# Attention of a decoder trunk: ScalarE takes all its parts of a projection's bank and of a turned bank first, then VectorE its own

## The chip, the cores and the metric

One core of a Trainium2 chip runs the whole kernel. The metric is the device time of one execution in microseconds, lower is better. A core has five engines with queues of their own that run in order: TensorE (PE), VectorE (DVE), ScalarE (ACT), GpSimd (POOL) and SyncE (SP, which here issues DMAs). They wait for each other by semaphores.

## The reference

One layer of a hybrid decoder trunk: 1024 tokens, model width 1024, float32. A normed input is projected for three groups of heads (a short convolution, attention of 8 heads of 64, a spatial gating MLP); their outputs go through `w_out`, then come a feed-forward MLP with squared ReLU (4096 wide) and a gated per-layer input. The part that matters here is the attention, which has no softmax:

```
q, k: RMSNorm per head of the projected columns; v as projected
z = einsum('bqhd,bkhd->bhqk', q, k) * scale          # scale = 64 ** -0.5
log_beta = log_sigmoid(z)
log_rem  = where(causal, log_sigmoid(-z), 0)         # strictly causal
suffix   = cumsum(log_rem, reverse=True) - log_rem
weights  = where(causal, exp(log_beta + suffix), 0)
o = einsum('bhqk,bkhd->bqhd', weights, v)
```

## The kernel before

Every float32 operand of a large product is split into a high part (rounded by ScalarE) and a low part (source minus high, by VectorE): `split`, L135 to L143. A product is three matmuls, high by high, high by low and low by high (L165 to L167).

**Order.** The program is written as generators that are woven together: attention of one pair of heads with the projection of the next, in the ratio of their matmuls (`weave`); a short piece can be queued to come some units of work later (`later`). On top of that a scheduler built into the framework simulates the program and sets the order of each engine's queue from it. So moving a line can move what stands around it on every engine.

**Stages** (us of the profiled execution): input, gating and its weights up to about 76; the projection of the first head pair to about 117; attention woven with the projections of pairs 1 to 3 up to about 330; attention of the last pair woven with the convolution to about 420; out-projection to about 505; then the feed-forward MLP and the gate to the end.

**`project(pr)`**, L343 to L391. For each of the 8 tiles of 128 tokens, 24 matmuls write q, k and v of two heads into one PSUM bank, `qkv_ps` (128x384). These banks come from `ps_mm`, which has two, so the matmuls of a tile wait until the tile two before it has been read out. The readers are, in the order of the lines: ScalarE squares q and k (L374, tile `qk_sq`, or `sq`), VectorE sums the squares (`ss`, L377), GpSimd raises them to the power -1/2 (`rs`, L174 in a helper), VectorE scales q and k (`qk`, L382), then ScalarE takes v's high part (`V`, L141 in `split`) and VectorE its low part (L142). The last one frees the bank. Where engines read one bank after another, semaphores between them keep that order.

**`turn_qk`**, L393 to L417, queued after every second tile: transposes of `qk` into a bank of `ps_tr` (`qk_tr`; three banks, shared with the transposed weights `w_tr`), which is read out as q's high part (`QS`, ScalarE), q's low part (`q_lo`, VectorE), k's high part (`KH`, ScalarE, L405) and k's low parts of the two heads (`KL`, VectorE, L407, twice).

**`attend(pr)`**, L421 to L523. `stick`: for each block of 128 queries, z by three kinds of matmul (L447 with KH, L449 with KL, L453 for the mask) into banks of `ps_z` (two), two sigmoids on ScalarE (`rem` L454, `wt` L455), a running product on VectorE (a scan of up to 1024 elements, L459), and weights `wt` times `rem` (L462; on VectorE for the blocks 3, 5 and 7, on GpSimd for the rest). `gather`: the weights are transposed (`w_tr`, L484), split (`wT_hi` on ScalarE, `wT_lo` on VectorE, L138 and L139) and multiplied with V (`av`, L502). Each head has four groups `g` of two blocks; the two heads of a pair run them upwards, then downwards, so that the largest groups of the two heads meet.

Of the kernel before, what the change touches and what calls it, by code (L numbers as in the profile page):

```python
# [8 lines left out]
F32R = mybir.dt.float32r  # L9
AF = mybir.ActivationFunctionType  # L10
ALU = mybir.AluOpType
AX = mybir.AxisListType

P = 128
# [4 lines left out]
HD = 64  # L19
# [13 lines left out]
def hybrid_block(ctx: ExitStack, tc: tile.TileContext, a: dict):  # L33
# [5 lines left out]
    nc = tc.nc  # L39
# [17 lines left out]
    def name(s):  # L57
        n_of[0] += 1
        return f"{s}_{n_of[0]}"

    def slot(s, dt=F32, shape=(P, HT)):
        return sp.tile(list(shape), dt, tag="slot", name=name(s))
# [16 lines left out]
    def half_tmp(s, shape=(P, 256)):  # L79
        return tp.tile(list(shape), F32, tag="half", name=name(s), bufs=3)  # L80

    def bank(pool, s):
        return pool.tile([P, HT], F32, tag=pool.name, name=name(s))
# [4 lines left out]
    def wide_bank(s):  # L88

        turn_of[0] ^= 1  # L90
        return bank((ps_mm, ps_z)[turn_of[0]], s)
# [3 lines left out]
    def block(t):  # L95

        return t // 4, slice(t % 4 * P, (t % 4 + 1) * P)
# [21 lines left out]
    def load_const(key, shape):  # L119
        t = const.tile(list(shape), F32, name=f"c_{key}")  # L120
        nc.gpsimd.dma_start(t, a[key])
        return t
# [6 lines left out]
    gq = load_const("gq", [P, 1])  # L129
# [5 lines left out]
    def split(src, hi, lo, scale=None, low=nc.vector):  # L135

        if scale is None:
            last_hi[0] = nc.scalar.copy(hi, src)  # L138
            low.tensor_tensor(out=lo, in0=src, in1=hi, op=ALU.subtract)  # L139
        else:  # L140
            nc.scalar.activation(hi, src, AF.Copy, scale=scale)  # L141
            nc.vector.scalar_tensor_tensor(out=lo, in0=src, scalar=scale, in1=hi,  # L142
                                           op0=ALU.mult, op1=ALU.subtract)  # L143

    def load_w(src, cols, low=nc.vector):

        st = stage(src, cols)
        hi = wp.tile([P, 384], F32R, tag="w", name=name("whi"))
        lo = wp.tile([P, 384], F32R, tag="w", name=name("wlo"))
        split(st, hi[:, :cols], lo[:, :cols], low=low)  # L150
        return hi, lo
# [9 lines left out]
    def product(ps, terms, first=True, last=True):  # L161


        for i, ((lh, ll), (rh, rl)) in enumerate(terms):
            nc.tensor.matmul(ps, lh, rh, start=first and i == 0, stop=False)  # L165
            nc.tensor.matmul(ps, lh, rl, start=False, stop=False)  # L166
            done = nc.tensor.matmul(ps, ll, rh, start=False, stop=last and i == len(terms) - 1)  # L167
        return done

    def cols(parts, sl):  # L170
        return parts[0][:, sl], parts[1][:, sl]

    def power_mhalf(out, in_, n):
        last_power[0] = nc.gpsimd.tensor_tensor(out=out, in0=in_, in1=mhalf[:, :n], op=ALU.pow)  # L174
# [40 lines left out]
    ms1e, r1, r1h = [], [], []  # L215
# [27 lines left out]
    def later(units, piece):  # L243

        waiting.append((emitted[0] + units, piece))
# [97 lines left out]
    def project(pr):  # L343

        wk = [load_w(a["w_qkv"][pr, k], 384, nc.gpsimd if pr and k % 2 == 0 else nc.vector)
              for k in range(KT)]

        QS = [[None, None], [None, None]]

        KH = [[None, None], [None, None]]  # L350
        KL = [[None, None], [None, None]]
        V = [None] * 4
        low_q = [None, None]
        heads[pr] = QS, KH, KL, V, low_q
        for t in range(KT):
            th, ts = block(t)
            if t % 4 == 0:
                for hh, other in enumerate((hi_p, lo_p)):
                    KL[hh][th] = slot("KL", F32R)
                    nc.gpsimd.memset(KL[hh][th][other].bitcast(F32), 0.0)  # L360
                KH[0][th] = slot("KH", F32R)
                QS[0][th] = slot("QS", F32R)
                low_q[th] = slot("q_lo", F32R)
                QS[1][th] = slot("QS", F32R)
                KH[1][th] = slot("KH", F32R)
            ps = bank(ps_mm, "qkv_ps")[:, :384]
            for k0 in range(0, KT, 2):
                product(ps, [(cols(xn[k][th], ts), wk[k]) for k in (k0, k0 + 1)],
                        k0 == 0, k0 == KT - 2)
                yield 18  # L370

            sq = half_tmp("qk_sq", (P, 4, HD + 1))
            nc.scalar.copy(sq[:, :, HD], ms1e[t].broadcast_to([P, 4]))
            nc.scalar.activation(sq[:, :, :HD], ps[:, :256].rearrange("p (h d) -> p h d", d=HD),  # L374
                                 AF.Square, scale=HD ** -0.5)
            ss = small.tile([P, 4], F32, tag="ss", name=name("ss"))
            nc.vector.tensor_reduce(out=ss, in_=sq, axis=AX.X, op=ALU.add)  # L377
            rs = small.tile([P, 4], F32, tag="rs", name=name("rs"))
            power_mhalf(rs, ss, 4)
            if t % 2 == 0:  # L380
                qk = tp.tile([P, 2, 256], F32, tag="qk", name=name("qk"), bufs=2)
            nc.vector.tensor_tensor(  # L382
                out=qk[:, t % 2].rearrange("p (h d) -> p h d", d=HD),
                in0=ps[:, :256].rearrange("p (h d) -> p h d", d=HD),
                in1=rs.unsqueeze(2).broadcast_to([P, 4, HD]), op=ALU.mult)
            if t % 2 == 0:
                V[t // 2] = slot("V", F32R, (P, 2, 2, 2, HD))
            v = V[t // 2][:, t % 2]
            split(ps[:, 256:].rearrange("p (h d) -> p h d", d=HD), v[:, :, 0], v[:, :, 1], scale=r1[t])
            if t % 2 == 1:  # L390
                later(72, lambda t=t, qk=qk: turn_qk(heads[pr], t, qk))  # L391

    def turn_qk(head, t, qk):  # L393

        QS, KH, KL, _, low_q = head
        th = t // 4
        tr = bank(ps_tr, "qk_tr")
        for i in range(2):
            for j in range(2):
                o = j * 256 + i * P  # L400
                nc.tensor.transpose(tr[:, o:o + P], qk[:, i, j * P:(j + 1) * P], ident)
        ws = slice((t % 4 - 1) * P, (t % 4 + 1) * P)

        split(tr[:, :256], QS[0][th][:, ws], low_q[th][:, ws], scale=gq)
        nc.scalar.activation(KH[0][th][:, ws], tr[:, 256:], AF.Copy, scale=gk)  # L405
        for hh, own in enumerate((lo_p, hi_p)):
            nc.vector.scalar_tensor_tensor(out=KL[hh][th][own, ws], in0=tr[own, 256:],  # L407
                                           scalar=gk[own], in1=KH[0][th][own, ws],
                                           op0=ALU.mult, op1=ALU.subtract)
        if t % 4 == 3:  # L410
            nc.scalar.copy(KH[1][th][hi_p], KH[0][th][hi_p])
            nc.scalar.copy(KH[1][th][lo_p], KH[0][th][hi_p])
            nc.scalar.copy(KH[0][th][hi_p], KH[0][th][lo_p])
            nc.vector.tensor_copy(QS[1][th][hi_p], QS[0][th][hi_p])
            nc.vector.tensor_copy(QS[1][th][lo_p], low_q[th][hi_p])
            nc.vector.tensor_copy(QS[0][th][hi_p], low_q[th][lo_p])
        return 8  # L417
# [263 lines left out]
    for n in range(KT):  # L681
# [5 lines left out]
        for h in range(2):  # L687
            ps = wide_bank("pp_ps")
# [4 lines left out]
    for _ in normalize(1):  # L693
        pass
    alone = stream(gating(), project(0))
    fill = stream(project(1), project(2), project(3), convolve())
    for _ in alone:
        pass
# [48 lines left out]
    ps = ctx.enter_context(tc.tile_pool(name="ps", bufs=8, space=PSUM, reuse_waits="tile"))  # L747

    def late_slot(tag, s, dt=F32):
        return late.tile([P, HT], dt, tag=tag, name=name(s), bufs=LATE[tag])  # L750
# [172 lines left out]
    for h in range(2):  # L923
        for n in (0, 4, 1, 5, 2, 6, 3, 7):
# [28 lines left out]
            t = hg[n][h] = late_slot("tmp", "hg")  # L953
# [29 lines left out]
    for i in range(FT):  # L983
# [16 lines left out]
        v = late_slot("tmp", "v")  # L1000
# [104 lines left out]
    def residual(n, h):  # L1105
        if h_res[n][h] is None:
            h_res[n][h] = slot("h")
            nc.sync.dma_start(h_res[n][h], h_dram[n, h])
        return h_res[n][h]
# [28 lines left out]
    for s, (c, p, j) in enumerate(steps):  # L1138
# [13 lines left out]
        elif p == 6:  # L1152
            subtract(nc.vector, u_sum[j], u_sum[j], bank)
            if last:
                add(nc.vector, h_res[j][1], h_res[j][1], u_sum[j])
                for h in range(2):
                    t = residual(j + 4, h)
                    subtract(nc.vector, t, t, u_sum[j])
        elif p in (2, 3):
            t = residual(j, p - 2)  # L1160
# [3 lines left out]
        else:  # L1164
            h = 0 if p == 4 else 1
            t = residual(j + 4, h)
# [55 lines left out]
    for p in GATE:  # L1222
        for j in range(4):
# [14 lines left out]
            for bank, c in zip(banks, cs):  # L1238
# [8 lines left out]
                elif p == 5:  # L1247
                    e_of[j] = late_slot("tmp", "e")
                    add(nc.vector, e_of[j], bank, v_of[j])
                    t = late_slot("tmp", "gt")  # L1250
                    add(nc.vector, t, d_bank.pop((3, j))[0], e_of[j])
                    gated(j, 1, t, t, c, by_dma=True)
                elif p == 7:
                    t = e_of[j][:, c]
                    add(nc.vector, t, bank, t)
                    gated(j + 4, 1, t, t, c, -1.0, True)
                elif p == 4:
                    t = v_of[j][:, c]
# [84 lines left out]
```

## Time and profile before

| | before |
|---|---|
| time, median of 3 runs (range) | 1217.78 us (1216.59 to 1219.84) |
| the profiled execution: time, span | 1216.81 us, 1214.9 us |
| mean granted TensorE clock | 0.993 |
| DMA moved, mean rate | 254.04 MB, 209 GB/s |

The span runs from the first to the last instruction. The rows of the profile name an instruction by its engine, line, operation and tiles (output, then inputs); a row of the timeline gives start, duration and, in brackets, the idle time ahead of it with the instruction that ended it. L numbers are lines of the kernel before; in the kernel after, lines from 394 to 404 are 4 higher and later ones 6 higher.

### The profile page before, as it was taken

What the parts mean: (1) busy time and instruction counts of PE and PEld (TensorE: products, weight loads), DVE (VectorE), ACT (ScalarE), POOL (GpSimd) and SP (SyncE); (2) the same over time, 40 slices, a digit from 0 to 9 for tenths busy, and PEclk for the clock granted to TensorE, in tenths of its full rate; (3) what the DMA queues carried; (4) which work ended last, traced back from release to release, by engine and by line L of the source; (5) the groups of instructions that cost most, each with busy time, mean ns of one, the idle gap of its engine ahead of it and who ended that gap; (6) DMA issues with size and microseconds to landing.
All of it is one profiled execution on the core that took longest, in us unless ns stands there. A gap on an engine that the chain in (4) does not pass through costs nothing.

```text
span 1214.9 us, 17743 instructions
## 1 busy us (share of the span) xinstructions
PE 1191.8 (98%) x5852; PEld 1018.2 (84%) x5852; DVE 886.8 (73%) x1310; ACT 629.1 (52%) x1244; POOL 400.9 (33%) x408
## 2 busy tenths in 40 slices
PE   9999899999999999999999999999999999999997
PEld 7899899898988888888888888888888888888886
DVE  7846888988887657877878768787665556753597
ACT  7736767667764355744333333356443444546542
POOL 3324345365343312124453544421023301013412
PEclk9999999999999999999999999999999999999998
DMA  9602359999554786779999899778889985654857
GB/s 318 222 18 94 124 166 267 247 184 171 132 116 101 164 287 207 198 194 269 251 256 251 231 261 258 217 249 277 321 248 313 279 264 171 217 163 112 179 160 208
DMA packets 127964, 254.04 MB, mean 209 GB/s; under 512 B 14496, under 2 KB 22432, under 8 KB 127168
## 3 DMA queue, kind: packets, MB, share of 16 engines
q1 hardware_dynamic: 94992, 168.08, 41.8%
q0 software_dynamic: 27664, 57.05, 25.0%
q10 hardware_dynamic: 5216, 27.79, 6.4%
q8 instruction: 46, 0.75, 0.2%
q14 instruction: 46, 0.38, 0.1%
HBM read 192.30 MB, written 92.80 MB: 235 GB/s over the span
## 4 chain that ended last, share of the span: by engine, by line
PE 86%; DVE 5%; DMA 4%; POOL 1%; issue 1%; ACT 1%; SPq 0%; ACTq 0%; DVEq 0%; POOLq 0%
PE f_ps L812 25%; PE d_ps L812 25%; PE g_ps L812 6%; PE qkv_ps L165 3%; PE qkv_ps L166 3%; PE qkv_ps L167 3%; PE av L502 2%; PE w_tr L484 2%; DVE rem L459 1%; PE vu_ps L167 1%; PE vu_ps L166 1%; PE vu_ps L165 1%; PE o_ps L167 1%; PE o_ps L165 1%; PE o_ps L166 1%
## 5 line engine op out<-in xcount | busy, mean ns | idle before, releaser
L139 DVE TENSOR_TENSOR w_lo<-raw,w_hi 128x512 fp32r<-128x512 f32 x280 | 245.1, 879 | 88.1 <-ACT w_hi L138 86.4
L138 ACT CAST w_hi<-raw 128x512 fp32r<-128x512 f32 x280 | 171.9, 619 | 232.6 <-PE d_ps L812 112.6
L812 PE MATMUL f_ps<-hn_hi,w_hi 128*128 128x512 f32 x448 | 175.1, 392 | 0.0
L812 PE MATMUL d_ps<-f_hi,w_hi 128*128 128x512 f32 x448 | 174.8, 390 | 0.0
L812 PE MATMUL f_ps<-hn_lo,w_hi 128*128 128x512 f32 x448 | 174.7, 390 | 0.0
L812 PE MATMUL f_ps<-hn_hi,w_lo 128*128 128x512 f32 x448 | 174.5, 390 | 0.0
L812 PE MATMUL d_ps<-f_hi,w_lo 128*128 128x512 f32 x448 | 174.3, 389 | 0.0
L812 PE MATMUL d_ps<-f_lo,w_hi 128*128 128x512 f32 x448 | 174.3, 389 | 0.0
L459 DVE TENSOR_TENSOR_SCAN rem<-rem 128x128 f32<-128x128 f32 (+3 forms) x64 | 90.2, 1420 | 23.0 <-ACT rem L454 22.9
L812 PEld LDWEIGHTS f_ps<-hn_lo,w_hi 128*128 128x128 f32 x448 | 84.4, 188 | 17.9 <-issue 0.2
L812 PEld LDWEIGHTS f_ps<-hn_hi,w_hi 128*128 128x128 f32 x448 | 84.5, 189 | 17.6 <-issue 0.2
L812 PEld LDWEIGHTS f_ps<-hn_hi,w_lo 128*128 128x128 f32 x448 | 84.4, 188 | 17.7
L812 PEld LDWEIGHTS d_ps<-f_hi,w_hi 128*128 128x128 f32 x448 | 84.1, 188 | 17.7 <-issue 0.2
L812 PEld LDWEIGHTS d_ps<-f_lo,w_hi 128*128 128x128 f32 x448 | 84.1, 188 | 17.6 <-issue 0.2
L812 PEld LDWEIGHTS d_ps<-f_hi,w_lo 128*128 128x128 f32 x448 | 84.1, 188 | 17.5
L165 PE MATMUL qkv_ps<-whi,xn_hi 128*128 128x384 f32 x256 | 90.4, 353 | 0.1
L167 PE MATMUL qkv_ps<-whi,xn_lo 128*128 128x384 f32 x256 | 87.8, 343 | 0.0
L166 PE MATMUL qkv_ps<-wlo,xn_hi 128*128 128x384 f32 x256 | 87.6, 342 | 0.0
L139 DVE TENSOR_TENSOR f_lo<-raw,f_hi 128x512 fp32r<-128x512 f32 x112 | 77.0, 718 | 12.6 <-ACT f_hi L138 12.2
L138 ACT CAST f_hi<-raw 128x512 fp32r<-128x512 f32 x112 | 67.0, 620 | 28.9 <-DMA raw<-f_dram 25.9
L798 POOL TENSOR_TENSOR S<-S,sq 128x512 f32<-128x512 f32 x19 | 27.4, 1440 | 157.8 <-ACT sq L874 157.8
L174 POOL TENSOR_TENSOR rs<-ss,mhalf 128x4 f32<-128x4 f32 x32 | 40.1, 1253 | 83.1 <-DVE ss L377 83.1
(252 smaller groups left out, 2704.4 us busy)
## 6 DMA issues: line engine op xcount, KB each, us to landing
raw<-in_w_ff SPq DMA_DIRECT2D x148, 256.0 KB, 4.1
raw<-f_dram SPq DMA_DIRECT2D x112, 256.0 KB, 5.1
raw<-w_sums SPq DMA_DIRECT2D x64, 256.0 KB, 3.9
f_dram<-f SPq DMA_DIRECT2D x48, 256.0 KB, 4.0
f_dram<-t SPq DMA_DIRECT2D x48, 256.0 KB, 3.7
w_sums<-in_w_ff POOLq DMA_DIRECT2D x8, 1024.0 KB, 11.6
w_sums<-w_sums POOLq DMA_DIRECT2D x8, 1024.0 KB, 13.0
raw<-in_w_out SPq DMA_DIRECT2D x28, 256.0 KB, 3.9
```

What stands on the lines that cost most here:

```text
L138: last_hi[0] = nc.scalar.copy(hi, src)
L139: low.tensor_tensor(out=lo, in0=src, in1=hi, op=ALU.subtract)
L165: nc.tensor.matmul(ps, lh, rh, start=first and i == 0, stop=False)
L166: nc.tensor.matmul(ps, lh, rl, start=False, stop=False)
L167: done = nc.tensor.matmul(ps, ll, rh, start=False, stop=last and i == len(terms) - 1)
L174: last_power[0] = nc.gpsimd.tensor_tensor(out=out, in0=in_, in1=mhalf[:, :n], op=ALU.pow)
L459: nc.vector.tensor_tensor_scan(out=back, data0=back, data1=back, initial=1.0, op0=ALU.mult, op1=ALU.bypass)
L484: nc.tensor.transpose(tr[:, n:n + P], wts[i][:, kb * P:(kb + 1) * P], ident)
L502: nc.tensor.matmul(av[:, first * P:], lhs, part[:, o:o + m], start=kb == 0 and part is hi, stop=kb == 2 * g + 1 and part is lo)
L798: return eng.tensor_tensor(out=out, in0=x, in1=y, op=ALU.add)
L812: done = nc.tensor.matmul(bank, l, r, start=first and k == 0 and i == 0, stop=k == len(b) - 1 and i == 2, skip_group_check=True)
```

## The change

In `project`, v's high part (ScalarE) and then the squares come first; VectorE follows with v's low part and the sum of the squares, and `qk` is now the bank's last reader. In `turn_qk`, ScalarE takes `QS` and `KH` one behind the other, then VectorE takes `q_lo` and both `KL`. The instructions and their operands are the same, and so is their number on every engine.

```diff
--- before.py
+++ after.py
@@ -369,10 +369,18 @@
                         k0 == 0, k0 == KT - 2)
                 yield 18
 
+            if t % 2 == 0:
+                V[t // 2] = slot("V", F32R, (P, 2, 2, 2, HD))
+            v = V[t // 2][:, t % 2]
+            ps_v = ps[:, 256:].rearrange("p (h d) -> p h d", d=HD)
+            nc.scalar.activation(v[:, :, 0], ps_v, AF.Copy, scale=r1[t])
+
             sq = half_tmp("qk_sq", (P, 4, HD + 1))
             nc.scalar.copy(sq[:, :, HD], ms1e[t].broadcast_to([P, 4]))
             nc.scalar.activation(sq[:, :, :HD], ps[:, :256].rearrange("p (h d) -> p h d", d=HD),
                                  AF.Square, scale=HD ** -0.5)
+            nc.vector.scalar_tensor_tensor(out=v[:, :, 1], in0=ps_v, scalar=r1[t], in1=v[:, :, 0],
+                                           op0=ALU.mult, op1=ALU.subtract)
             ss = small.tile([P, 4], F32, tag="ss", name=name("ss"))
             nc.vector.tensor_reduce(out=ss, in_=sq, axis=AX.X, op=ALU.add)
             rs = small.tile([P, 4], F32, tag="rs", name=name("rs"))
@@ -383,10 +391,6 @@
                 out=qk[:, t % 2].rearrange("p (h d) -> p h d", d=HD),
                 in0=ps[:, :256].rearrange("p (h d) -> p h d", d=HD),
                 in1=rs.unsqueeze(2).broadcast_to([P, 4, HD]), op=ALU.mult)
-            if t % 2 == 0:
-                V[t // 2] = slot("V", F32R, (P, 2, 2, 2, HD))
-            v = V[t // 2][:, t % 2]
-            split(ps[:, 256:].rearrange("p (h d) -> p h d", d=HD), v[:, :, 0], v[:, :, 1], scale=r1[t])
             if t % 2 == 1:
                 later(72, lambda t=t, qk=qk: turn_qk(heads[pr], t, qk))
 
@@ -401,8 +405,10 @@
                 nc.tensor.transpose(tr[:, o:o + P], qk[:, i, j * P:(j + 1) * P], ident)
         ws = slice((t % 4 - 1) * P, (t % 4 + 1) * P)
 
-        split(tr[:, :256], QS[0][th][:, ws], low_q[th][:, ws], scale=gq)
+        nc.scalar.activation(QS[0][th][:, ws], tr[:, :256], AF.Copy, scale=gq)
         nc.scalar.activation(KH[0][th][:, ws], tr[:, 256:], AF.Copy, scale=gk)
+        nc.vector.scalar_tensor_tensor(out=low_q[th][:, ws], in0=tr[:, :256], scalar=gq,
+                                       in1=QS[0][th][:, ws], op0=ALU.mult, op1=ALU.subtract)
         for hh, own in enumerate((lo_p, hi_p)):
             nc.vector.scalar_tensor_tensor(out=KL[hh][th][own, ws], in0=tr[own, 256:],
                                            scalar=gk[own], in1=KH[0][th][own, ws],
```

What this does to the queues, at three places. The numbers behind a tile's name tell its copies apart; they are given in order of building, so one that belongs to a moved line can differ by a few between the kernels.

**VectorE, where the largest groups of the first head pair meet.** `qkv_ps_1606` and `qkv_ps_1723` are the two projection banks that are held there, `qk_tr_1684` the turned bank, `rem` with 1024, 896 and so on the scans. Before (`qk` of bank 1606 stands six rows above this piece):

```order
L459 SCALAR_TENSOR_TENSOR rem_1613<-rem_1613 128x1024
L382 TENSOR_TENSOR qk_1718<-qkv_ps_1723,rs_1799 128x256
L142 SCALAR_TENSOR_TENSOR q_lo_1411<-qk_tr_1684,c_gq,QS_1410 128x256
L462 TENSOR_TENSOR wt_1614<-wt_1614,rem_1613 128x1023
L459 SCALAR_TENSOR_TENSOR rem_1696<-rem_1696 128x896
L407 SCALAR_TENSOR_TENSOR KL_1405<-qk_tr_1684,c_gk,KH_1409 64x256
L407 SCALAR_TENSOR_TENSOR KL_1407<-qk_tr_1684,c_gk,KH_1409 64x256
L142 SCALAR_TENSOR_TENSOR V_1720<-qkv_ps_1606,r_569,V_1720 128x2x64
L142 SCALAR_TENSOR_TENSOR V_1720<-qkv_ps_1723,r_569,V_1720 128x2x64
L459 SCALAR_TENSOR_TENSOR rem_1730<-rem_1730 128x1024
L139 TENSOR_TENSOR wT_lo_1757<-w_tr_1751,wT_hi_1756 128x512
L462 TENSOR_TENSOR wt_1731<-wt_1731,rem_1730 128x1023
```

After (ahead of this piece stand the scan `rem_1613`, `wt_1614`, `wT_lo_1663`, `q_lo_1411` and `KL_1405`):

```order
L413 SCALAR_TENSOR_TENSOR KL_1407<-qk_tr_1684,c_gk,KH_1409 64x256
L465 SCALAR_TENSOR_TENSOR rem_1696<-rem_1696 128x896
L139 TENSOR_TENSOR wT_lo_1757<-w_tr_1751,wT_hi_1756 128x512
L382 SCALAR_TENSOR_TENSOR V_1711<-qkv_ps_1606,r_569,V_1711 128x2x64
L385 TENSOR_REDUCE ss_1717<-qk_sq_1713 128x4
L382 SCALAR_TENSOR_TENSOR V_1711<-qkv_ps_1723,r_569,V_1711 128x2x64
L385 TENSOR_REDUCE ss_1799<-qk_sq_1795 128x4
L465 SCALAR_TENSOR_TENSOR rem_1730<-rem_1730 128x1024
L139 TENSOR_TENSOR wT_lo_1772<-w_tr_1766,wT_hi_1771 128x512
L468 TENSOR_TENSOR wt_1731<-wt_1731,rem_1730 128x1023
L139 TENSOR_TENSOR wT_lo_1787<-w_tr_1781,wT_hi_1786 128x512
L390 TENSOR_TENSOR qk_1721<-qkv_ps_1606,rs_1719 128x256
```

The low parts of k moved ahead of the scan of 896. The sums `ss`, which stood ahead of the scan `rem_1613`, stand behind the scan of 896, and `qk`, which now frees the bank 1606, behind the next scan of 1024 and its weights. On ScalarE, V of these two banks stands behind the copy `y_both_1694` in both kernels; the squares, which stood 20 rows ahead of it, now stand right behind V.

**TensorE, at the same place.** `qkv_ps_1813` is the next tile of the projection, into the bank of 1606. Before:

```order
L484 MATMUL w_tr_1781<-ident,wt_1582 128x128
L484 MATMUL w_tr_1781<-ident,wt_1614 128x128
L484 MATMUL w_tr_1781<-ident,wt_1582 128x128
L484 MATMUL w_tr_1781<-ident,wt_1614 128x128
L165 MATMUL qkv_ps_1813<-whi_1359,xn_hi_462 128x384
L166 MATMUL qkv_ps_1813<-wlo_1360,xn_hi_462 128x384
L167 MATMUL qkv_ps_1813<-whi_1359,xn_lo_463 128x384
```

After:

```order
L490 MATMUL w_tr_1781<-ident,wt_1582 128x128
L490 MATMUL w_tr_1781<-ident,wt_1614 128x128
L490 MATMUL w_tr_1781<-ident,wt_1582 128x128
L490 MATMUL w_tr_1781<-ident,wt_1614 128x128
L508 MATMUL av_87<-wT_hi_1756,V_983 128x256
L508 MATMUL av_87<-wT_lo_1757,V_983 128x256
L508 MATMUL av_87<-wT_hi_1756,V_983 128x256
L508 MATMUL av_87<-wT_lo_1757,V_983 128x256
L490 MATMUL w_tr_1820<-ident,wt_1582 128x128
L490 MATMUL w_tr_1820<-ident,wt_1614 128x128 x2
L453 MATMUL z_1857<-KH_957,QS_1159 128x512
L455 MATMUL z_1857<-KL_951,QS_1159 128x512
```

Behind the same transposes `w_tr_1781` the tile of the projection came at once; now 30 matmuls of the attention (transposes `w_tr`, z and av, the first of them shown) come between. In the second head pair the like tile has 29 matmuls more ahead of it; in the third its place is the same.

**TensorE, where attention begins.** `z_1349`, `z_1423`, `z_1439` and `z_1449` are the first four blocks of the first head, `qkv_ps_1214`, `1249` and `1296` tiles of the first head pair's projection. Before:

```order
L165 MATMUL qkv_ps_1249<-whi_945,xn_hi_523 128x384
L166 MATMUL qkv_ps_1249<-wlo_946,xn_hi_523 128x384
L167 MATMUL qkv_ps_1249<-whi_945,xn_lo_524 128x384
L447 MATMUL z_1349<-KH_953,QS_954 128x128
L449 MATMUL z_1349<-KL_949,QS_954 128x128
L453 MATMUL z_1349<-below,ident 128x128
L447 MATMUL z_1423<-KH_953,QS_954 128x256
L449 MATMUL z_1423<-KL_949,QS_954 128x256
L453 MATMUL z_1423<-below,ident 128x128
L401 MATMUL qk_tr_1274<-ident,qk_1209 128x128 x2
L165 MATMUL qkv_ps_1296<-whi_903,xn_hi_462 128x384
L166 MATMUL qkv_ps_1296<-wlo_904,xn_hi_462 128x384
```

After (ahead of it stands the last matmul of `qkv_ps_1214`, behind it `qkv_ps_1249`):

```order
L453 MATMUL z_1349<-KH_953,QS_954 128x128
L455 MATMUL z_1349<-KL_949,QS_954 128x128
L459 MATMUL z_1349<-below,ident 128x128
L453 MATMUL z_1423<-KH_953,QS_954 128x256
L455 MATMUL z_1423<-KL_949,QS_954 128x256
L459 MATMUL z_1423<-below,ident 128x128
L453 MATMUL z_1439<-KH_953,QS_954 128x384
L455 MATMUL z_1439<-KL_949,QS_954 128x384
L459 MATMUL z_1439<-below,ident 128x128
L453 MATMUL z_1449<-KH_953,QS_954 128x512
L455 MATMUL z_1449<-KL_949,QS_954 128x512
L459 MATMUL z_1449<-below,ident 128x128
```

The first two z blocks stood behind the tile `qkv_ps_1249` and the other two behind the next; now all four stand ahead of `qkv_ps_1249`. Of the 5,800 rows of TensorE, the last 2,891 are the same in both kernels.

## The prediction

> **What bounds the kernel now.** I read the page first, then busy time by stretch of the span, then TensorE's waits in the attention stretch, then the timelines of VectorE and TensorE around the longest of them.
>
> ```profile
> PE 1191.8 (98%) x5852; PEld 1018.2 (84%) x5852; DVE 886.8 (73%) x1310; ACT 629.1 (52%) x1244; POOL 400.9 (33%) x408
> ```
>
> Busy time by stretch (columns: stretch, its length, then busy time of PE, PEld, DVE, ACT and POOL, granted clock, DMA share, GB/s):
>
> ```profile
> 76.00:117.00 41.00, 40.87 (x253) 40.35 (x253) 21.29 (x52) 20.83 (x56) 14.59 (x17) 1.00 0.13 45
> 117.00:330.00 213.00, 202.68 (x1293) 191.65 (x1292) 182.09 (x279) 146.91 (x371) 105.23 (x102) 0.98 0.75 186
> ```
>
> TensorE is the bound: 1191.8 of 1214.9 us. What the change can move is its idle time and its clock. From 117 to 330 us attention of one head pair is woven with the projection of the next; there TensorE idles 213 - 202.7 = 10.3 us and VectorE is busy 182.1, so VectorE is the second bound. TensorE's waits from 76 to 420 us name it (total, times, longest):
>
> ```profile
> PE w_tr L484 <- DVE KL L407: 4.6, 3, 1.7
> PE w_tr L484 <- DVE wt L462: 2.8, 4, 1.2
> ```
>
> The first row is one stall for each of three head pairs, at about 149, 217 and 287 us, where the longest attention blocks meet. The first, on VectorE and on TensorE:
>
> ```profile
> 142.78 0.56 DVE L139 TENSOR_TENSOR wT_lo<-w_tr,wT_hi 128x384 fp32r<-128x384 f32 x1 [0.42 <-ACT wT_hi L138]
> 143.28 2.29 DVE L459 TENSOR_TENSOR_SCAN rem<-rem 128x1024 f32<-128x1024 f32 x1
> 145.48 0.40 DVE L382 TENSOR_TENSOR qk<-qkv_ps,rs 128x256 f32<-128x256 f32 x1
> 145.80 0.47 DVE L142 SCALAR_TENSOR_TENSOR q_lo<-qk_tr,c_gq,QS 128x256 fp32r<-128x256 f32 x1
> 146.19 1.21 DVE L462 TENSOR_TENSOR wt<-wt,rem 128x1023 f32<-128x1023 f32 x1
> 147.32 2.02 DVE L459 TENSOR_TENSOR_SCAN rem<-rem 128x896 f32<-128x896 f32 x1
> 149.26 0.97 DVE L407 SCALAR_TENSOR_TENSOR KL<-qk_tr,c_gk,KH 64x256 fp32r<-64x256 f32 x2
> 150.26 0.61 DVE L142 SCALAR_TENSOR_TENSOR V<-qkv_ps,r,V 128x128 fp32r<-128x128 f32 x2
> 150.79 2.64 DVE L459 TENSOR_TENSOR_SCAN rem<-rem 128x1024 f32<-128x1024 f32 x1
> 153.35 0.66 DVE L139 TENSOR_TENSOR wT_lo<-w_tr,wT_hi 128x512 fp32r<-128x512 f32 x1
> 153.93 1.21 DVE L462 TENSOR_TENSOR wt<-wt,rem 128x1023 f32<-128x1023 f32 x1
> 155.06 1.27 DVE L139 TENSOR_TENSOR wT_lo<-w_tr,wT_hi 128x512 fp32r<-128x512 f32 x2
> 156.95 1.49 DVE L459 TENSOR_TENSOR_SCAN rem<-rem 128x640 f32<-128x640 f32 x1 [0.62 <-ACT rem L454]
> ```
>
> ```profile
> 150.29 1.11 PE L484 MATMUL w_tr<-ident,wt 128*128 128x128 f32 x4 [1.14 <-DVE KL L407]
> 151.06 0.67 PE L165 MATMUL qkv_ps<-whi,xn_hi 128*128 128x384 f32 x1
> ```
>
> The transposes w_tr need the turned bank that KL (L407) still reads. KL waits for nothing but its place: behind wt and the scan of 896. When it ends at 150.23, w_tr starts, and right behind come the V parts, which free the projection's bank for qkv_ps at 151.06. Each stall also costs clock:
>
> ```profile
> 146.84:150.25 3.41, 1.42 (x9) 1.05 (x9) 3.36 (x4) 3.41 (x10) 0.74 (x1) 1.00 0.00 0
> 150.25:153.66 3.41, 3.37 (x12) 3.37 (x13) 3.40 (x4) 0.98 (x2) 1.03 (x1) 0.50 0.00 0
> ```
>
> ```profile
> 218.53:221.94 3.41, 3.28 (x12) 3.28 (x13) 3.38 (x5) 0.77 (x2) 2.15 (x2) 0.50 1.12 206
> 286.77:290.18 3.41, 1.72 (x11) 1.72 (x12) 3.35 (x6) 2.31 (x6) 2.50 (x3) 1.00 1.12 204
> ```
>
> After a stretch of 3.41 us in which TensorE was 42% busy (1.42) it got clock 0.50 for the next 3.41 us, which loses about 1.7 us; this comes twice. In the third place it was 50% busy (1.72) and kept its clock.
>
> **The change, part by part.** No instruction comes or goes; only places in the queues move. The profiled execution took 1216.81 us, 0.97 below the median of 1217.78. Sums below stand against 1216.81, and 0.97 is added at the end.
>
> Turned bank. KH no longer waits for VectorE's q_lo, and KL now stands ahead of the scan of 896. In the first cluster VectorE's pieces, by start-to-start of the rows above, are scan 1024 2.20, wt 1.13, wT_lo 0.50, q_lo 0.39, KL 1.00. The scan can start about 142.6, as the wT_lo of 0.50, and some of the idle 0.42 ahead of that, no longer stand before it (143.28). So KL ends at 142.6 + 5.2 = 147.8 instead of 150.23: **the 1.1 us that w_tr waited for it go**, and so do the other two stalls.
>
> What is late next is the projection's bank. Before, its last reader was V's low part, with ScalarE's V waiting for qk (15.1 us in all, off TensorE's path); now it is qk, behind ss and rs. Groups from 117 to 330 us (busy us in all, mean ns of one, then the idle time ahead and its releaser):
>
> ```profile
> L377 DVE TENSOR_REDUCE ss<-qk_sq 128x4 f32<-128x260 f32 x24 | 9.9, 411 | 1.0 <-ACT qk_sq L374 1.0
> ```
>
> ```profile
> L141 ACT ACTIVATE V<-qkv_ps,r 128x128 fp32r<-128x128 f32 x25 | 9.2, 371 | 15.2 <-DVE qk L382 15.1
> ```
>
> ```profile
> L174 POOL TENSOR_TENSOR rs<-ss,mhalf 128x4 f32<-128x4 f32 x25 | 33.0, 1322 | 59.9 <-DVE ss L377 59.9
> ```
>
> The ScalarE square stays behind V, which stands where it stood before, so ss moves from ahead of the scans to behind the scan of 896, and qk, which needs GpSimd's rs 1.32 later, drops behind the next scan of 1024 and its wt. From KL's end VectorE runs scan 896 1.94, wT_lo 0.58, two V 0.53, two ss 0.82, scan 1024 2.56, wT_lo 0.58, wt 1.13, wT_lo 0.58, qk 0.40, in all 9.1 us: **the bank comes free at 156.9 instead of 151.06**. Meanwhile TensorE has what the order now puts ahead of qkv_ps: 30 attention matmuls.
>
> ```profile
> 155.66 0.39 PE L447 MATMUL z<-KH,QS 128*128 128x512 f32 x1
> 155.89 0.40 PE L449 MATMUL z<-KL,QS 128*128 128x512 f32 x1
> ```
>
> ```profile
> 159.38 0.28 PE L502 MATMUL av<-wT_hi,V 128*128 128x256 f32 x1
> 159.49 0.28 PE L502 MATMUL av<-wT_lo,V 128*128 128x256 f32 x1
> ```
>
> Pitches: 0.23 for a z of 512, less for narrower ones, 0.11 to 0.12 for an av, and a w_tr taken at 0.11. 13 av 1.6, 7 w_tr 0.8, 10 z 1.6: 4.0 us. Before, TensorE worked without a gap from 150.9 to 156.9, less 1.4 for the half clock to 153.66: 4.6 us of work. **First cluster: +0.6.** Bounds: 0, if the 30 start earlier still and the bank comes 0.6 sooner; 2.3, if the clock halves again (1.7). Behind a waiting qkv_ps stands all of TensorE's queue, so nothing fills the gap.
>
> Second cluster:
>
> ```profile
> 218.66 1.11 PE L484 MATMUL w_tr<-ident,wt 128*128 128x128 f32 x4 [1.71 <-DVE KL L407]
> 219.43 0.67 PE L165 MATMUL qkv_ps<-whi,xn_hi 128*128 128x384 f32 x1
> ```
>
> Here qk also falls behind a scan of 640 (1.4 by its row). Its stall lies 68.4 us after the first one's (218.66 - 150.29), so its scan of 1024 starts at 211.0. The same pieces and this one sum to 15.7: free at 226.7 instead of 219.43. Before, 7.3 us less 1.3 of half clock (to 221.94) were work, 6.0; now 29 matmuls of the same kinds, 4.0. **+2.0**; bounds 0.6 (bank 1.5 sooner, as some VectorE work may already lie earlier) and 3.7 with a half clock.
>
> Third cluster:
>
> ```profile
> 288.46 0.66 PE L484 MATMUL w_tr<-ident,wt 128*128 128x128 f32 x4 [1.73 <-DVE KL L407]
> 288.88 0.42 PE L165 MATMUL qkv_ps<-whi,xn_hi 128*128 128x384 f32 x1
> ```
>
> There qk stands right behind the scan of 896. It lies 138.2 after the first, its scan of 1024 starts at 280.8, and 2.20, q_lo 0.39, KL 1.00, wt 1.13, V and ss 1.35, scan 1.94 and qk 0.40 are 8.4: free at 289.2 instead of 288.88. **+0.3**, bounds 0 and, with a first half clock there, 2.0.
>
> Start of attention. All four first z blocks now stand ahead of a tile of 24 projection matmuls; ps_z has two banks.
>
> ```profile
> 108.88 0.22 PE L447 MATMUL z<-KH,QS 128*128 128x128 f32 x1
> ```
>
> ```profile
> 109.08 0.39 ACT L374 ACTIVATE qk_sq<-qkv_ps 128x256 f32<-128x256 f32 x1 [1.64 <-PE qkv_ps L167]
> 109.48 1.28 ACT L454 ACT_TABLE_LOAD   x1
> 110.78 0.28 ACT L454 ACTIVATE rem<-z 128x128 f32<-128x128 f32 x1
> 110.95 0.27 ACT L455 ACTIVATE wt<-z 128x128 f32<-128x128 f32 x1
> ```
>
> The third z needs ScalarE through V 0.37 (as long as the square), square 0.40, table load 1.30 and two sigmoids, 0.17 and 0.27, after the tile's end, 2.5; six small z matmuls at about 0.11 cover 0.6. TensorE waits 1.9 and, with the fourth z, about 2.1; the projection matmuls behind cannot pass. Against it the longest wait for wt, 1.2, goes, as the weights start a tile earlier. **+0.9**, bounds -1.2 (the scheduler's place finds the bank free) and 2.3.
>
> At nothing: the reorder where projections run alone, 76 to 117 us, since V, square, ss, rs, qk (0.37 + 0.39 + 0.41 + 1.32 + 0.40 = 2.9 us) lie under the other bank's 24 matmuls (40.87 us for 253 there, so 3.9 us); without that cover each tile could cost those 2.9. The feed-forward part is at nothing too: its TensorE rows, the last 2,891, keep their order.
>
> Sum: 0.9 + 0.6 + 2.0 + 0.3 = +3.8 without a new half clock: 1220.6, and with 0.97 **1221.6 us**.
>
> [...]
>
> **The rivals.**
> (1) Cure, faster: KL was the only thing late, and the bank is never waited for because TensorE's attention matmuls wait for VectorE no longer. Then 4.6 and two half clocks of 1.7 go: 1216.8 - 8.0 + 1.0 = **1209.8**. It decides if the bank is free by the time the 30 matmuls end, near 152. For it: KL really moves up. Against: VectorE's rows have no gap from 142.78 to 156.3, so moving one piece up moves another down.
> (2) The wait only changes place: the extra work TensorE finds ahead of the bank equals what it lost, and the z wait is hidden. Within 0.3%, **1217.8**. For it: equal counts, and a TensorE 98% busy either way.
> (3) The change does not do what it says: in some tiles the scheduler leaves ScalarE's V as late as before (it does, in the clusters). That is built into the forecast; if it were so of KL too, the time is that of (2).
> (4) Half clocks follow again. TensorE would be 4.0 of 9.1 us (147.8 to 156.9) busy (44%) in the first cluster and 4.0 of 10.5 (38%; 216.2 to 226.7) in the second, near the 42% that lost the clock and below the 50% that kept it. One adds 1.7, two 3.4, three 5.1: 1223.3 to **1226.7**.
>
> **How the numbers follow.** Forecast (1219.2 to 1223) 0.36; cure 0.17; no change, (2) and (3), 0.27; half clocks 0.20. A measurement of this kernel tells about 0.3% from no change, 3.65 us: 1214.1 and 1221.4. Faster takes the cure, 0.17; slower takes the half clocks and six tenths of the forecast, 0.42; the rest, 0.41, is the same. The range, 1211 to 1228, cuts most of the cure, 0.12 or so, and reaches past three half clocks to all upper bounds together (2.3 + 2.3 + 3.7 + 2.0 = +10.3, 1228.1). The forecast's own range with rival 4 is 1219.2 to 1226.7.
>
> **What would show it.** Right: w_tr waits for KL shrink to under 1 us in all; new TensorE waits of qkv_ps for qk near 153 to 157 and 223 to 227 us; z waits about 2 us for ScalarE's wt near 105 to 107; V on ScalarE no longer waits for qk (15.1 us in this stretch before). Wrong: qkv_ps near 151 and 219 as before, or clock 1.00 throughout 140 to 300 with TensorE's idle time under 6 us, would mean the cure; a wait on av or z in place of qkv_ps means the cluster's limit is VectorE's whole load and not this order.

## The result, and the profile after

The change makes the kernel slower: 1233.56 us (median of 4 runs, 1233.11 to 1235.95) against 1217.91 (1216.59 to 1219.84) of the kernel before, a ratio of 1.0131, 95% interval 1.0112 to 1.0150. That is 15.7 us, where +3.8 was forecast and 1228 was the upper end of the range.

The page of the kernel after, busy time of the engines:

```profile
span 1233.9 us, 17792 instructions
...
PE 1199.9 (97%) x5852; PEld 1025.5 (83%) x5852; DVE 885.2 (72%) x1310; ACT 626.2 (51%) x1244; POOL 400.4 (32%) x408
```

The instruction counts and the busy times of VectorE, ScalarE and GpSimd are those of before; TensorE, with the same instructions, is busy 8 us longer and idle 11 us longer. The profiled execution took 1235.95 us, 2.4 over the median, so its rows add up to 19 us and not to 15.7.

Where the loss came is seen by following the same events in both kernels: the first scan of 1024 in the stretches where the largest groups of a head pair meet (called clusters below; the first starts at 143.28 before), and the first matmul of the out-projection. Timelines, before:

```profile
211.67 2.29 DVE L459 TENSOR_TENSOR_SCAN rem<-rem 128x1024 f32<-128x1024 f32 x1
281.45 2.29 DVE L459 TENSOR_TENSOR_SCAN rem<-rem 128x1024 f32<-128x1024 f32 x1
420.32 0.47 PE L165 MATMUL o_ps<-y_hi,wo_hi 128*128 128x512 f32 x1 [0.62 <-DVE cv_acc L661]
```

After:

```profile
147.31 2.47 DVE L465 TENSOR_TENSOR_SCAN rem<-rem 128x1024 f32<-128x1024 f32 x1
222.01 2.47 DVE L465 TENSOR_TENSOR_SCAN rem<-rem 128x1024 f32<-128x1024 f32 x1
294.12 2.29 DVE L465 TENSOR_TENSOR_SCAN rem<-rem 128x1024 f32<-128x1024 f32 x1
439.46 0.47 PE L165 MATMUL o_ps<-y_hi,wo_hi 128*128 128x512 f32 x1 [1.01 <-DVE cv_acc L667]
```

The kernel after is 4.0 us late at the first cluster, 10.3 at the second, 12.7 at the third and 19.1 at the out-projection; behind that, nothing is added (spans 1214.9 and 1233.9). So the loss lies ahead of the out-projection, in each part of the attention; 1.0 of the first 4.0 us comes from ahead of the attention, as is shown below.

TensorE's waits from 76 to 440 us (total, times, longest):

```profile
PE av L508 <- DVE wT_lo L139: 8.9, 6, 2.0
PE z L453 <- ACT wt L461: 5.3, 5, 2.1
PE w_tr L490 <- DVE wt L468: 4.6, 3, 1.5
PE qk_tr L405 <- DVE qk L390: 1.8, 1, 1.8
```

The waits of `w_tr` for KL, 4.6 us before, are gone as the change meant. In their place TensorE waits for its own attention: for the low parts of the weights, the sigmoids, the weights. It does not wait for the projection's bank. And its clock halves often; stretches of the kernel after with their granted clock (0.50):

```profile
108.59:112.00 3.41, 3.41 (x12) 3.16 (x11) 3.29 (x5) 2.04 (x6) 2.73 (x3) 0.50 0.68 231
156.37:163.20 6.83, 5.57 (x23) 4.89 (x21) 6.83 (x9) 4.17 (x11) 5.24 (x3) 0.50 0.00 0
231.47:238.30 6.83, 6.44 (x24) 6.00 (x25) 6.83 (x9) 3.78 (x10) 4.78 (x5) 0.50 1.13 207
299.73:306.56 6.83, 5.37 (x18) 4.84 (x19) 5.59 (x6) 5.65 (x15) 5.07 (x6) 0.50 1.13 211
385.07:388.48 3.41, 3.41 (x12) 2.73 (x11) 3.41 (x7) 2.51 (x6) 1.37 (x2) 0.50 1.10 193
```

Before, two windows of 3.41 us in this part had half the clock; now eight have (27.3 us, in which TensorE is busy 24.2). The whole part, before and after:

```profile
76.00:420.00 344.00, 331.38 (x2013) 305.25 (x2012) 270.77 (x419) 212.08 (x521) 154.90 (x148) 0.99 0.63 154
```

```profile
76.00:439.00 363.00, 340.52 (x2017) 313.54 (x2016) 271.69 (x420) 209.45 (x522) 155.36 (x148) 0.96 0.60 146
```

Idle time of TensorE grew from 12.6 to 22.5 us (+9.9), and its busy time by 9.1 us for the same work: about half of the loss is waiting, half is clock.

Cover is what independent matmuls of the projection give: work for TensorE while the attention waits for other engines. What is missing of it is seen by the projection's matmuls alone. Busy time of the instructions on `qkv_ps` in the first cluster, before (columns without GpSimd):

```profile
138.00:142.00 4.00, 1.39 (x7) 1.07 (x6) 0.42 (x1) 0.38 (x1) 1.00 0.54 184
142.00:146.00 4.00, 0.00 (x0) 0.00 (x0) 0.40 (x1) 0.00 (x0) 1.00 0.00 0
146.00:150.00 4.00, 0.00 (x0) 0.00 (x0) 0.00 (x0) 0.64 (x2) 1.00 0.00 0
150.00:154.00 4.00, 2.94 (x10) 3.02 (x11) 0.61 (x2) 0.00 (x0) 0.57 0.00 0
```

After:

```profile
142.00:146.00 4.00, 2.35 (x12) 1.61 (x10) 0.00 (x0) 0.00 (x0) 1.00 0.70 262
146.00:150.00 4.00, 0.00 (x0) 0.00 (x0) 0.00 (x0) 0.00 (x0) 1.00 0.02 4
150.00:154.00 4.00, 0.00 (x0) 0.00 (x0) 0.00 (x0) 1.19 (x4) 1.00 0.00 0
154.00:158.00 4.00, 0.00 (x0) 0.00 (x0) 0.69 (x2) 0.00 (x0) 0.80 0.00 0
158.00:162.00 4.00, 0.00 (x0) 0.00 (x0) 0.41 (x1) 0.00 (x0) 0.50 0.00 0
```

Taken from one projection matmul's start to the next, the largest gaps were 12.0, 10.3 and 11.6 us in the three clusters, and are 18.2, 18.5 and 13.0 now. In such a gap TensorE has only transposes and matmuls of the attention, and its longest waits above are for VectorE and ScalarE.

### The profile page after: what moved, and what is told of

Read it like the earlier page. It is cut to its first block, busy times and chain, and to the rows that moved or that the text cites. A ratio compares the mean times of both kernels' runs of the same rounds, so it can differ in the third digit from the quotient of the medians.

```text
span 1233.9 us, 17792 instructions
## 1 busy us (share of the span) xinstructions
PE 1199.9 (97%) x5852; PEld 1025.5 (83%) x5852; DVE 885.2 (72%) x1310; ACT 626.2 (51%) x1244; POOL 400.4 (32%) x408
## 4 chain that ended last, share of the span: by engine, by line
PE 90%; DVE 4%; ACT 2%; DMA 2%; issue 1%; POOL 0%; SPq 0%; DVEq 0%; ACTq 0%; POOLq 0%
PE f_ps L818 25%; PE d_ps L818 25%; PE g_ps L818 6%; PE qkv_ps L165 4%; PE qkv_ps L166 3%; PE qkv_ps L167 3%; PE av L508 2%; PE o_ps L165 2%; PE o_ps L167 2%; PE o_ps L166 2%; PE w_tr L490 2%; DVE rem L465 1%; PE z L453 1%; PE vu_ps L167 1%; PE vu_ps L166 1%; PE vu_ps L165 1%
## 5 line engine op out<-in xcount | busy, mean ns | idle before, releaser
L465 DVE TENSOR_TENSOR_SCAN rem<-rem 128x128 f32<-128x128 f32 (+3 forms) x64 | 93.8, 1472 | 31.2 <-ACT rem L460 30.9
L468 POOL TENSOR_TENSOR wt<-wt,rem 128x127 f32<-128x127 f32 (+4 forms) x40 | 47.2, 1218 | 85.8 <-DVE rem L465 67.2
```

The lines of the kernel that those rows point to most:

```text
L465: nc.vector.tensor_tensor_scan(out=back, data0=back, data1=back, initial=1.0, op0=ALU.mult, op1=ALU.bypass)
L468: done = (nc.vector if on_vector else nc.gpsimd).tensor_tensor(out=wt[:, :W - 1], in0=wt[:, :W - 1], in1=rem[:, 1:W], op=ALU.mult)
```

## The experiments

All times are medians, with the ratio to the kernel before on the same chip and its interval. The kernel before took 1217.26 us in the first group, 1216.50 in the second and 1216.14 in the third. "The change" is the kernel after.

**First group: which half, and which order.** Three theories: A, ScalarE's V stands late in its queue, the squares now stand behind it, and so the projection's bank is freed late; B, KL ahead of VectorE's scans holds up the weights; C, any move costs, because the order was settled.

`project_alone` is the change with the old reading of the turned bank:

```diff
-        nc.scalar.activation(QS[0][th][:, ws], tr[:, :256], AF.Copy, scale=gq)
+        split(tr[:, :256], QS[0][th][:, ws], low_q[th][:, ws], scale=gq)
         nc.scalar.activation(KH[0][th][:, ws], tr[:, 256:], AF.Copy, scale=gk)
-        nc.vector.scalar_tensor_tensor(out=low_q[th][:, ws], in0=tr[:, :256], scalar=gq,
...
```

> Only the change in the projection (V, then the squares on ScalarE; V's low part, then ss on VectorE; qk last); the turned bank is read as before. Theory A (V stands late on ScalarE, the squares now queue behind it, so the projection's bank is freed late and its matmuls are missing as cover for the attention): nearly the whole loss, 1229 to 1236 us. Theory B (KL and q_lo ahead of VectorE's scans hold up the weights): no loss, 1216 to 1220. Theory C (any move of the order costs): 1222 to 1234.

1235.10 us (1230.72 to 1238.94), 1.0137 [1.0100, 1.0174]: the new projection alone brings the whole loss.

`turn_alone` is the kernel before with only the second half of the diff, the new `turn_qk`.

> Only the change in the turned bank (QS, KH, then q_lo and KL); the projection as before. Theory A: no loss, the three waits of w_tr for KL go, 1212 to 1219 us. Theory B: 1229 to 1236. Theory C: 1222 to 1234.

1213.01 us (1212.16 to 1215.38), 0.9972 [0.9960, 0.9984]: faster than before. B falls, and so does C.

`squares_first` is the change with the squares ahead of V:

```diff
-            nc.scalar.activation(v[:, :, 0], ps_v, AF.Copy, scale=r1[t])
 
             sq = half_tmp("qk_sq", (P, 4, HD + 1))
...
                                  AF.Square, scale=HD ** -0.5)
+            nc.scalar.activation(v[:, :, 0], ps_v, AF.Copy, scale=r1[t])
+            ss = small.tile([P, 4], F32, tag="ss", name=name("ss"))
+            nc.vector.tensor_reduce(out=ss, in_=sq, axis=AX.X, op=ALU.add)
             nc.vector.scalar_tensor_tensor(out=v[:, :, 1], in0=ps_v, scalar=r1[t], in1=v[:, :, 0],
                                            op0=ALU.mult, op1=ALU.subtract)
-            ss = small.tile([P, 4], F32, tag="ss", name=name("ss"))
-            nc.vector.tensor_reduce(out=ss, in_=sq, axis=AX.X, op=ALU.add)
```

> The change with one order turned round: on ScalarE the squares come before V, on VectorE ss before V's low part; qk is still the last to read the bank, and the turned bank is read as in the change. Theory A: the loss goes, 1212 to 1220 us. Theory B: it stays, 1229 to 1236. Theory C: 1222 to 1234.

1212.04 us (1211.19 to 1213.03), 0.9960 [0.9944, 0.9976]: this small reordering turns a loss of 15.7 us into a gain of 5.2, and makes it **faster than both kernels**. Here `qk` is still the last reader of the bank. Its timeline in the first cluster, TensorE and VectorE:

```profile
150.74 0.45 PE L165 MATMUL qkv_ps<-whi,xn_hi 128*128 128x384 f32 x1 [1.70 <-DVE qk L390]
```

```profile
142.27 0.42 DVE L383 TENSOR_REDUCE ss<-qk_sq 128x4 f32<-128x260 f32 x1 [0.59 <-ACT qk_sq L379]
143.21 2.29 DVE L465 TENSOR_TENSOR_SCAN rem<-rem 128x1024 f32<-128x1024 f32 x1
...
150.27 0.41 DVE L390 TENSOR_TENSOR qk<-qkv_ps,rs 128x256 f32<-128x256 f32 x1
```

Here `ss` stands ahead of the scan of 1024, and `qk` ends 7.5 us after that scan's start (150.68 less 143.21), ahead of the next scan of 1024; the change needs 14.4. And here TensorE does wait for the bank, 1.7 us, as the prediction had it for the change.

`squares_first_old_turn` is the same with the old reading of the turned bank.

> As squares_first, with the turned bank read as before the change. Theory A: the loss goes, and the waits of w_tr for KL are back, 1215 to 1222 us. Theory B: 1216 to 1220. Theory C: 1222 to 1234.

1221.03 us (1217.17 to 1223.91), 1.0029 [1.0014, 1.0044]. The halves do not add: the new `turn_qk` gains 4.3 us on the old projection and 9.0 on this one, and this projection without it is 3.8 us slower than the kernel before. The waits of `w_tr` for KL are back in its profile (4.4 us, in three waits); what else makes up the difference no run shows.

**Second group: ScalarE's order or VectorE's, and the start of attention.** `squares_behind_v_only` is the change with `ss` ahead of V's low part on VectorE; ScalarE keeps V ahead of the squares.

```diff
-            nc.vector.scalar_tensor_tensor(out=v[:, :, 1], in0=ps_v, scalar=r1[t], in1=v[:, :, 0],
-                                           op0=ALU.mult, op1=ALU.subtract)
             ss = small.tile([P, 4], F32, tag="ss", name=name("ss"))
             nc.vector.tensor_reduce(out=ss, in_=sq, axis=AX.X, op=ALU.add)
+            nc.vector.scalar_tensor_tensor(out=v[:, :, 1], in0=ps_v, scalar=r1[t], in1=v[:, :, 0],
+                                           op0=ALU.mult, op1=ALU.subtract)
```

> The change with VectorE's order alone turned round (ss ahead of V's low part); ScalarE still takes V ahead of the squares. If ScalarE's order carries the loss (the squares wait behind V in its queue): 1229 to 1237 us. If VectorE's order does (ss behind V's low part): 1211 to 1219. Together with squares_first, which turned both round, this splits the two.

1231.42 us (1230.61 to 1233.97), 1.0129 [1.0108, 1.0151]: ScalarE's order carries the loss without VectorE's. The reverse, VectorE's order alone, was not run.

`third_z_later` is the change with the first four z blocks of the first head tied to the ends of projection tiles. By its trace the first two stay where the change has them, and the third and fourth go behind the tile where they stood before:

```diff
+                    with ExitStack() as pin:
+                        if pr == 0 and hh == 0 and t < 4:
+                            pin.enter_context(tc.issue_after(tile_end[0, 5 + t // 2].ins))
...
```

> The change with the third and fourth z block of the first head held back behind later tiles of the projection, as they stood before the change; nothing else moves. If the start of attention costs what its rows show (a wait of 2.05 us for the sigmoids and a half clock of 3.41 us behind it, 1.7): 1229 to 1231 us. If that time is given back later, because the weights then come later too: 1232 to 1235.

1231.60 us (1231.21 to 1237.09), 1.0142 [1.0109, 1.0174]. The wait at 108 us is gone from its profile (z for the sigmoids: 1.3 us in all, 5.3 in the change), and the mean granted clock is 0.989 (0.985 in the change), but other waits grew, `qkv_ps` for `qk` to 3.9 us. Of these, 2.75 us lie at 108.72, where the change waited for the sigmoids (up to 108.10): there TensorE now waited for the bank instead. The 2 us less than the change's 1233.56 lie inside the spread: this run does not settle how much of the start's cost comes through.

`qk_then_v_low` is `squares_first` with V's low part moved behind `qk` on VectorE.

> As squares_first, but VectorE takes V's low part last, behind qk (ScalarE: squares, V; the turned bank as in the change). If only the place of the squares matters, as squares_first, 1210 to 1215 us. If it matters that qk is the last reader (V's low part done while GpSimd works on rs), 2 to 6 us slower than squares_first, 1214 to 1219.

1213.85 us (1211.57 to 1215.50), 0.9977 [0.9965, 0.9989]. This lies in the first range, 0.15 us below the second, and 1.8 us from `squares_first`: which of the two reads the bank last matters little.

**Third group: why V stands late.** V's tile is one of 56 slots that many tensors share. `v_own_pool` gives V seven tiles of its own; the room is taken from the staged weights and loads. `less_staging` is its control, with the same smaller staging and V in the slots; two more kernels are the same pair for `squares_first`.

```diff
+    vpool = front.enter_context(tc.tile_pool(name="vpool", bufs=7))
...
-                V[t // 2] = slot("V", F32R, (P, 2, 2, 2, HD))
+                V[t // 2] = vpool.tile([P, 2, 2, 2, HD], F32R, tag="v", name=name("V"))
...
-STAGES = 7
-WBUFS = 20
+STAGES = 3
+WBUFS = 16
```

> The change, with V in a pool of its own of 7 tiles instead of the 56 shared slots; the room is taken from the staged weights (16 instead of 20 tiles) and the loads (3 stages instead of 7). To be compared with less_staging, which lacks only the pool. If V stands late because it must wait for a slot: 8 to 16 us faster than less_staging. If V is late for another reason, or the squares behind V cost anyway: within 4 us of it.

> The change with 16 tiles of staged weights instead of 20 and 3 load stages instead of 7, V in the shared slots: the control of v_own_pool. 1232 to 1245 us; the smaller staging alone may cost some us.

> squares_first with V in a pool of its own and the small staging of v_own_pool. If the slot matters only because the squares stand behind V: within 4 us of its control squares_first_less_staging, and within 4 us of v_own_pool, since then nothing waits behind V. If a late V costs in itself (through the bank that it holds): 5 us or more faster than the control.

> squares_first with the small staging and V in the shared slots, the control of squares_first_v_own_pool: 1212 to 1225 us.

| | V in the shared slots | V in its own pool |
|---|---|---|
| V, then squares (the change) | 1250.43 (1246.11 to 1254.36) | 1227.05 (1225.12 to 1230.70) |
| squares, then V | 1228.21 (1227.55 to 1231.28) | 1227.55 (1226.34 to 1229.62) |

The smaller staging costs 16 to 17 us by itself (1250.43 against 1233.56, 1228.21 against 1212.04), so both controls are slower than expected (1232 to 1245 and 1212 to 1225), and `v_own_pool` gains more over its control than the 8 to 16 us expected. Beside that, the table is plain: with a pool of its own the change gains 23.4 us, `squares_first` gains nothing that can be told (0.7), and the two orders then take the same time. At this staging the loss needs both: V in the shared slots, and the squares behind V. The pool also leaves the 56 slots to the other tensors, but that room gains `squares_first` nothing. ScalarE's timeline of the change in the first cluster:

```profile
152.23 0.38 ACT L517 COPY y_both<-av 128x256 f32<-128x256 f32 x1
152.50 0.38 ACT L376 ACTIVATE V<-qkv_ps,r 128x128 fp32r<-128x128 f32 x1
152.76 0.40 ACT L380 ACTIVATE qk_sq<-qkv_ps 128x256 f32<-128x256 f32 x1
```

V starts right behind `y_both`, with no idle time of its own: the late place in the queue is what the trace shows, and the slot, which the scheduler reckons with, is the reason by the table. The last matmul of the tile that these squares read ended at 139.39, 13.4 us earlier; in `squares_first` the like squares start 0.2 us behind their tile. In `v_own_pool` V stands ahead of `y_both`, 0.6 us behind the end of the tile's last matmul (149.44):

```profile
150.07 0.41 ACT L377 ACTIVATE V<-qkv_ps,r 128x128 fp32r<-128x128 f32 x1
150.33 0.43 ACT L381 ACTIVATE qk_sq<-qkv_ps 128x256 f32<-128x256 f32 x1
...
157.96 0.36 ACT L518 COPY y_both<-av 128x256 f32<-128x256 f32 x1
```

From 117 to 345 us its three longest gaps between projection matmuls are 5.3, 4.5 and 4.1 us; those of its control `less_staging` are 19.5, 10.6 and 7.0.

## Why the prediction was wrong

**What held.** KL moved ahead and its three waits went. The bank's chain was sized rightly: from the start of the scan of 1024 to the end of `qk` I added up 14.3 us for the first cluster and 15.7 for the second. VectorE's rows of the first, after:

```profile
151.88 0.99 DVE L413 SCALAR_TENSOR_TENSOR KL<-qk_tr,c_gk,KH 64x256 fp32r<-64x256 f32 x2
152.90 2.03 DVE L465 TENSOR_TENSOR_SCAN rem<-rem 128x896 f32<-128x896 f32 x1
...
155.83 0.41 DVE L385 TENSOR_REDUCE ss<-qk_sq 128x4 f32<-128x260 f32 x1
...
156.75 2.28 DVE L465 TENSOR_TENSOR_SCAN rem<-rem 128x1024 f32<-128x1024 f32 x1
...
161.26 0.41 DVE L390 TENSOR_TENSOR qk<-qkv_ps,rs 128x256 f32<-128x256 f32 x1
```

161.67 less 147.31 is 14.4; in the second cluster, `qk` starting at 237.34, it is 15.7. In the third it is 9.9 us (294.12 to 303.99) where 8.4 was added up; VectorE sat idle there for 1.14 us, waiting for a sigmoid. The third z block waited 2.05 us for the sigmoids, where 1.9 to 2.1 was the term. And the cause named there, squares and `ss` queued behind a late V, is the one that the experiments bear out.

**The step that failed** is the price of the 30 attention matmuls ahead of the next projection tile: "13 av 1.6, 7 w_tr 0.8, 10 z 1.6: 4.0 us", as if they waited for nothing and only the bank came late. TensorE after:

```profile
153.61 0.36 PE L508 MATMUL av<-wT_hi,V 128*128 128x256 f32 x1
155.71 0.39 PE L508 MATMUL av<-wT_lo,V 128*128 128x256 f32 x1 [1.73 <-DVE wT_lo L139]
...
159.66 0.58 PE L508 MATMUL av<-wT_lo,V 128*128 128x256 f32 x1 [1.26 <-DVE wT_lo L139]
...
163.71 0.34 PE L165 MATMUL qkv_ps<-whi,xn_hi 128*128 128x384 f32 x1
```

The first of the 30 starts at 153.61 and the tile at 163.71: 10.1 us. Two of them wait for VectorE's low parts, 3.0 us together, and about two thirds of them run at half clock, from 156.37 to 163.20; the tile starts 2.0 us after its bank was free. The bank was early enough; the matmuls put ahead of the tile were not. From each cluster's first scan to the next of the events timed above, the terms were +0.6, +2.0 and +0.3, and 6.3, 2.3 and 6.5 us came (each of these holds the whole head pair behind its cluster, not the cluster alone). That the second is of the right size is luck: its term was a wait for the bank, and there, too, TensorE waited for a low part (1.85 us, up to 231.57) and lost two windows to the half clock, and not for the bank.

The prediction named this as a sign of being wrong: a wait on av or z in place of `qkv_ps` would mean that VectorE's whole load is the limit and not this order. The sign came, but that reading of it does not hold: `squares_first` gives VectorE the same instructions in another order and is 21.5 us faster than the change.

**The clock was put into a rival.** The half clocks had 0.20 and at most three windows; eight came, against two before. The busy shares of 44% and 38% reckoned for the clusters pointed to them, and the forecast still left them out. The first window at the start of attention was in no term.

**The start.** The term was +0.9. The wait for the sigmoids was priced rightly, the half clock behind it (3.41 us from 108.59, after 1.36 us busy of 3.41) was not priced, and the gain of 1.2 was met by a new wait, `qk_tr` for `qk`, of 1.78 us at 121.60. The kernel is 4.0 us late at the first cluster, 1.0 of it from ahead of the change: the wait for the first staged weights is 1.6 us in this execution, 0.6 in that of before.

**The last head pair** was put at nothing ("the feed-forward part is at nothing too" was right; for 330 to 420 us there was no term). There one av waits 1.8 us at 384.60, and a half clock follows at 385.07.

What stays open: how the 4.0, 6.3 and 6.5 us divide between the wait that starts them and the waits that follow from it, since `third_z_later` took away one such wait, priced together with the half clock behind it at 3.7 us by the rows of the change, and gained between nothing and about 2 us; which tensor holds the slot that V waits for; and what the place of the projection's tile costs by itself, as no run moved only the tile back ahead of the 30 matmuls.

## What to carry to other kernels

In a queue that runs in order, put ahead what needs nothing but the bank, and behind it what also needs a buffer from a shared pool: an instruction that stands late for want of a slot holds up all that stands behind it on its engine (here 1231.42 us with the squares behind V and 1212.04 with them ahead of it, with VectorE's lines in the same order). When filler work is moved out of a dependent stretch, price that stretch by its own chain from engine to engine, not by the busy time of its matmuls; here 4.0 us of matmuls, by the prediction's estimate, took 10. And where TensorE's busy share falls to about one half over 3.41 us, give the halved clock a term in the sum itself: of the kernel after, 1.34 to 1.68 us busy stood ahead of each of the five dips from 76 to 440 us, though 1.64 us kept its clock once.

## What the runs showed of the hardware

The granted clock halved behind a window with TensorE far from idle (1.68 us busy of 3.41), and once halved it stayed so through one that was far from empty (3.02 us busy). Windows of the kernel after:

```profile
152.96:156.37 3.41, 1.68 (x14) 1.48 (x13) 3.38 (x5) 2.40 (x8) 1.27 (x1) 1.00 0.00 0
```

```profile
149.54:152.96 3.42, 1.90 (x14) 1.56 (x14) 3.25 (x7) 3.04 (x8) 0.00 (x0) 1.00 0.00 0
```

```profile
231.47:234.88 3.41, 3.02 (x12) 2.81 (x13) 3.41 (x5) 2.50 (x7) 3.41 (x4) 0.50 1.13 208
234.88:238.30 3.42, 3.42 (x14) 3.18 (x13) 3.42 (x6) 1.28 (x3) 1.37 (x2) 0.50 1.13 207
```

1.68 us busy of 3.41 (49%) was followed by half the clock, 1.90 (56%) was not, and before the change 1.72 (50%) was not. At half clock, 3.02 us busy (88%) was followed by another window at half clock, and 3.42 by the full clock; before the change 3.28 us (96%, from 218.53) was followed by the full clock. Each dip in a cluster lasted two windows, 6.83 us, where those of before lasted one, 3.41.

The busy share draws no sharp line ahead of a half clock. In the kernel after, two windows of about the same busy time (48%) went different ways: the one from 118.83 (1.64 us) kept its clock, the one from 381.66 (1.63) lost it. And a window that the profile shows as full was followed by half the clock:

```profile
542.09:545.50 3.41, 3.41 (x29) 3.28 (x28) 3.20 (x6) 1.12 (x3) 0.00 (x0) 1.00 0.00 0
545.50:548.91 3.41, 3.41 (x10) 2.64 (x9) 3.41 (x8) 0.00 (x0) 1.69 (x2) 0.50 0.82 256
```

24 of the 29 matmuls in that window are only two columns wide (`ms_ps`, 128x2). So the busy time of the profile does not by itself tell which clock is granted next; what does, these runs do not show.
